# Moving the first factor of a low-rank gate out of a split weight stream

## The chip, the core and the metric

The kernel runs on one core of a Trainium2 chip. The metric is the time of one execution on the device, in microseconds (us). Of the kernel before there are three timed runs, 1939.54, 1939.91 and 1941.91 us, with a median of 1939.91 us, and one profiled execution.

The names used below are those of the profile. PE is TensorE, which multiplies matrices; PEld is its loading of the stationary operand. DVE is VectorE, ACT is ScalarE, POOL is GpSimd and SP is SyncE. SP computes nothing here, but most DMA transfers are issued from its queue, and a smaller part from POOL's. Each engine works through its own instructions in order.

## The reference: what is computed

One step of a decoder layer for 256 prompt rows and 8 sample rows, so 264 columns in all (`NT`), with a model width of 2048. All weights are float32. The input is normalised and modulated by a vector that depends on the conditioning input, giving `h`. One projection `z = h @ w_in` feeds three mixers. The third one, gated linear attention, takes from it queries, keys, values, an output gate and 16 columns `glr`, the first half of a low-rank gate:

```python
h = rmsnorm(x, g_pre_mix) * (1.0 + sc1) + sh1
z = h @ w_in                                   # 2048 x 15376
(z_uv, hq, hf, hi, hg, gq, gk, gv, gr, glr, z_gate) = split(z, offsets)
log_a = log_sigmoid(glr @ gla_w_up + gla_b_up) / GLA_TAU     # 16 -> 512 columns
```

`glr` stands at columns 9216 to 9231 of `w_in`; columns 9232 and on are the merge gates `z_gate`. The mixers' outputs are projected, merged by the gates and projected again, and a squared-ReLU MLP follows (2048 to 8192 and back).

## The kernel before, in words

Activations are kept transposed: 128 model channels on the partitions, the 264 rows as columns. A block is an SBUF buffer of the pool `b` with 28 of them; four channels' tiles of 128 x 264 fill one. `hh` and `hl` hold `h` split in two parts of a reduced float32 form (`fp32r` in the profile), whose sum is `h`; `xT[q]`, q from 0 to 3, holds the unsplit float32 `h` for channel tiles 4q to 4q+3, from which they are made.

**The weight stream.** Nearly all products go through class `Stream` and `granule`. A weight tile of 128 x 4 x 256 or the like is loaded by SP into a `raw` buffer (512 KB), split by ACT into `whi` (L109) and by DVE into `wlo` (L106), and used in three matmuls per 128 x 128 piece: high part by `hh` (L641), high part by `hl` (L642), low part by `hh` (L643), each with 264 columns. 24 of these are a granule. Loads run up to five granules ahead, splits two. `plan()` writes down the order of the weights once, and `zin(c0, width)` is a projection of `width` columns of `w_in` by this path. For `glr` the width is 128: `zin(9216, P)` computes the 16 wanted columns and 112 unwanted ones, in two granules of 24 matmuls.

**The first phase.** Until about 300 us the kernel works in five passes over 2, 2, 4, 4 and 4 of the 16 channel tiles (`CHUNKS`), because each next pass needs its part of the modulation vector first. That is a product of the conditioning rows with `w_ada` (class `First`, L294): plain float32 matmuls, four of them side by side in the array, each with a stationary operand of 32 columns and its own 32 output partitions. Their weights, 256 or 512 KB each, are loaded by SP into blocks. Later modulation vectors are computed likewise, by `rounds` (L362).

**The gate.** `gla_group()` runs after the first phase: two stream projections for queries, two for keys, `zin(9216, P)`, then four for the values, each followed by one plain float32 matmul for 128 columns of the gate (L1030, 16 rows deep: `gla_w_up` by the copied `lr`).

**The background.** The mixers themselves are generators. After each granule `background()` gives two queues of them an allowance (`rate`, set from `RATES` at the start of each stage), so that their small matmuls and their DVE and ACT work lie between the granules; `now` counts granules, and several waits of the sample part of the mixers are counted in it.

**Order.** On PE, SP and POOL the order is as written in the program; on DVE and ACT, in most stages, a scheduler sets it when the program is built, from its own estimates.

Of the kernel before, what the change touches and what calls it, by code (L numbers as in the profile page):

```python
# [15 lines left out]
P = 128  # L16
# [17 lines left out]
SPLIT_BUFS = 6  # L34
NBLK = 28
CHUNKS = (2, 2, 4, 4, 4)
RATES = ((1.8, 0.5), (1.6, 0.5), (1.25, 0.5), (1.0, 0.5))
ST_BUFS = 4
VB_BUFS = 2
N_PRE = 6  # L40
# [17 lines left out]
def hybrid_step_kernel(  # L58
# [27 lines left out]
    def blk(shape=None, dt=F32):  # L86
        shape = shape or [P, 4, NT]
        return blkp.tile(shape, dt, tag="b", name=nm("b"))
# [447 lines left out]
    def blocks(w, k0, nk, c0, width=CW):  # L536
        kc = min(nk, 1024 // width)
        return [(w, k0 + kb, kc, c0, width) for kb in range(0, nk, kc)]

    def plan():  # L540

        out, k0 = [], 0
        for n in CHUNKS:
            for gi in range(0, len(begin), 4 // n):
                out.append((win, k0, n, begin[gi][0], 4 // n * CW))
            k0 += n
        for c0 in (6144, 6400, 6656, 6912):
            out += blocks(win, 0, KT, c0)
        out += blocks(win, 0, KT, 9216, P)
        for s in range(4):  # L550
            out += blocks(win, 0, KT, 7168 + s * CW)
        for n in range(N_BRANCH):
            if n:
                g0 = 5120 if n == 1 else 8192
                for s in range(4):
                    out += blocks(win, 0, KT, g0 + s * CW)
            for m in range(8):
                out += blocks(win, 0, KT, 9232 + n * D + m * CW) + blocks(w_branch[0, n], 0, 8, m * CW)
        for m in range(8):
            out += blocks(w_out[0], 0, KT, m * CW)  # L560
        for f in range(NFB + 1):
            if f < NFB:
                if f == 0:
                    out += blocks(w_mlp_up[0], 0, KT, 0, 2 * CW)
                for m in range(0 if f else 2, FB // CW):
                    out += blocks(w_mlp_up[0], 0, KT, f * FB + m * CW)
            if f:
                for m in range(8):
                    out += blocks(w_mlp_down[0], (f - 1) * (FB // P), FB // P, m * CW)
        return out  # L570
# [217 lines left out]
    order.__exit__(None, None, None)  # L788
    order = tc.manual_schedule(engines=set(every[0:3]))
    order.__enter__()  # L790
    k0 = 0
    for ci, n in enumerate(CHUNKS):
        final = ci == len(CHUNKS) - 1
# [4 lines left out]
        for gi in range(ng):  # L798
# [12 lines left out]
                    S.activation(dst, dst, fn)  # L811
            if ci == 0 and 2 * gi + 8 < KT:
                x_transposed(2 * gi + 8)
            if not final:
                if ci or gi:
                    next(nxt, None)
            else:
                if gi % 4 == 0:
                    rounds.steps()
                    rounds.load()  # L820
                if gi % 3 == 0 and srcs_a:
                    const_a(srcs_a.pop(0))
# [188 lines left out]
    def gla_group():  # L1011
        G = Group()
        G.dv, G.i = 256, 2
        G.q, G.g, G.k, G.v = blk(), blk(), blk(), [blk(), blk()]
        wl = blk([16, 512 + NT])
        wup, lr = wl[:, 0:512], wl[:, 512:512 + NT]
        nc.gpsimd.dma_start(wup, gla_w_up[0])
        for s in range(2):
            z = zin(6144 + s * CW)
            S.copy(pair(G.q, s), z)  # L1020
        for s in range(2):
            z = zin(6656 + s * CW)
            S.activation(pair(G.k, s), z, AF.Copy, scale=GLA_SCALE)
        z = zin(9216, P)
        S.copy(lr, z[0:16, 0, :])
        for s in range(4):
            z = zin(7168 + s * CW)
            S.copy(pair(G.v[s // 2], s % 2), z)
            ps = sm()
            T.matmul(ps[:, 0:NT], wup[:, s * P:(s + 1) * P], lr, start=True, stop=True)  # L1030
            V.tensor_scalar(G.g[:, s, :], ps[:, 0:NT], bupT[:, s:s + 1], None, ALU.add)
        G.s_in = lambda b, h, n: state_gla[0, b, h:h + n].rearrange("h k v -> k h v")
        G.s_out = lambda b, h, n: gla_sample[0, b, h:h + n].rearrange("h k v -> k h v")
# [709 lines left out]
```

## Time and profile before

| quantity | value |
|---|---|
| median of three runs | 1939.91 us |
| the profiled execution's own time | 1938.26 us |
| its span, first to last instruction | 1936.5 us |
| PE busy | 1903.5 us, 98% of the span |
| DVE, ACT, POOL busy | 1186.6, 1002.7, 84.8 us |
| moved by DMA | 442.05 MB, mean 228 GB/s |

An x with a number behind it is a count of instructions. A plain float32 matmul is recorded twice in the trace, so that counts of them are double those of the program. A row of the timeline gives the start, the time from start to end of the whole row, the engine, the line, output and inputs, the shape (partitions by columns of the stationary operand, then the moving operand) and, in brackets, idle time before it and what ended it. Matmuls overlap: each of those of the stream lasts 0.28 us but starts 0.12 us after the one before it, so durations of single matmuls must not be added up; what one costs is seen from the starts.

### The profile page before, as it was taken

The page shows a single profiled execution, that of the slowest core. Times are in us where ns is not written, and L with a number is a line of the kernel's source. Part 1 is how long each engine was busy: PE and PEld are TensorE (multiplying, and loading weights), DVE is VectorE, ACT ScalarE, POOL GpSimd, SP SyncE. Part 2 cuts the span into 40 slices and gives each one's busy share as a digit, 9 for nine tenths or more (in the row PEclk, how much of TensorE's full clock was granted, in tenths as well). Part 3 has the DMA queues.
Part 4 walks back from the last instruction along what each step waited for, and adds up shares of the span by engine and source line. Part 5 has one row for each costly group of instructions (what it writes and reads, how often), then busy time and mean ns, then how long its engine had stood idle before and what let it go on. Part 6 is the DMA issues. An engine that isn't in the chain of part 4 may idle for free.

```text
span 1936.5 us, 42145 instructions
## 1 busy us (share of the span) xinstructions
PE 1903.5 (98%) x17012; PEld 1813.5 (94%) x17012; DVE 1186.6 (61%) x2092; ACT 1002.7 (52%) x1818; POOL 84.8 (4%) x146
## 2 busy tenths in 40 slices
PE   7999999999999999999999999999999999999998
PEld 5889999999999989899999989999999999999997
DVE  4566667686676784555555666545556555555665
ACT  5434454665855755544444555444444545454544
POOL 1000000001101111100000010000000000000000
PEclk9999999999999999999999999999999999999999
DMA  9897786778778778887777846676665656555552
GB/s 334 318 331 252 232 299 205 227 257 263 230 254 253 228 255 262 288 271 250 255 257 230 302 124 214 221 239 185 184 181 179 185 177 184 180 180 182 180 182 100
DMA packets 339395, 442.05 MB, mean 228 GB/s; under 512 B 14946, under 2 KB 281040, under 8 KB 339200
## 3 DMA queue, kind: packets, MB, share of 16 engines
q1 hardware_dynamic: 329136, 409.62, 65.8%
q0 software_dynamic: 8992, 28.48, 4.5%
q8 instruction: 133, 2.18, 0.4%
q10 hardware_dynamic: 1072, 1.25, 0.2%
q14 instruction: 62, 0.51, 0.1%
HBM read 427.60 MB, written 11.70 MB: 227 GB/s over the span
## 4 chain that ended last, share of the span: by engine, by line
PE 95%; DMA 3%; DVE 1%; ACT 1%; issue 0%; SPq 0%; POOL 0%; DVEq 0%; ACTq 0%
PE mm L641 29%; PE mm L642 28%; PE mm L643 28%; PE ada L362 3%; DMA b<-in_w_ada_dram 2%; PE ada L294 1%; DMA vbc<-vs_d 1%; PE sm L833 1%; PE sm L661 1%; PE sm L1190 1%; PE sm L668 1%; DMA b<-in_x_prompt_dram 0%; PE sm L1560 0%; DMA raw<-in_w_in_dram 0%; DVE wlo L106 0%
## 5 line engine op out<-in xcount | busy, mean ns | idle before, releaser
L641 PE MATMUL mm<-b,whi 128*128 128x264 f32 x4624 | 1325.2, 287 | 2.4 <-ACT b L109 1.6
L643 PE MATMUL mm<-b,wlo 128*128 128x264 f32 x4624 | 1311.9, 284 | 4.1 <-DVE wlo L106 2.6
L642 PE MATMUL mm<-b,whi 128*128 128x264 f32 x4624 | 1313.0, 284 | 1.9 <-issue 1.0
L106 DVE TENSOR_TENSOR wlo<-raw,whi 128x512 fp32r<-128x512 f32 x1136 | 776.7, 689 | 561.8 <-ACT whi L109 557.9
L109 ACT CAST whi<-raw 128x512 fp32r<-128x512 f32 x1136 | 696.1, 618 | 741.7 <-PE mm L642 654.8
L641 PEld LDWEIGHTS mm<-b,whi 128*128 128x128 f32 x4624 | 869.8, 188 | 44.7 <-issue 26.7
L643 PEld LDWEIGHTS mm<-b,wlo 128*128 128x128 f32 x4624 | 869.4, 188 | 6.2 <-DVE wlo L106 3.4
L642 PEld LDWEIGHTS mm<-b,whi 128*128 128x128 f32 x4624 | 869.7, 188 | 1.5 <-DVE b L106 1.2
L103 DVE TENSOR_TENSOR b<-b,mm 128x528 f32<-128x528 f32 (+1 forms) x137 | 95.7, 699 | 41.9 <-PE mm L643 41.7
L1087 DVE SCALAR_TENSOR_TENSOR st<-vbc,b,st 128x128 f32<-128x128 f32 (+1 forms) x96 | 34.2, 390 | 59.6 <-DMA vbc<-vs_d 56.2
L1085 ACT ACTIVATE st<-st,fs 128x128 f32<-128x128 f32 (+1 forms) x96 | 37.2, 431 | 53.9 <-DMA st<-in_state_hgrn_dram 27.2
L362 PE MATMUL ada<-araw,cT 128*32 128x512 f32 x296 | 39.8, 601 | 0.0
L294 PE MATMUL ada<-b,cT 128*32 128x256 f32 (+1 forms) x640 | 35.0, 353 | 3.2 <-DMA b<-in_w_ada_dram 3.0
L100 DVE TENSOR_TENSOR b<-b,b 128x512 f32<-128x512 f32 (+1 forms) x47 | 33.8, 740 | 1.3 <-ACT b L1203 1.1
L294 PEld LDWEIGHTS ada<-b,cT 128*32 128x32 f32 x640 | 17.8, 113 | 15.8 <-DMA b<-in_w_ada_dram 7.6
L1088 POOL DMA_DIRECT2D out_dram<-st x32 | 23.5, 735 | 127.7 <-DVE st L1087 122.9
L362 PE MATMUL ada<-b,cT 128*32 128x512 f32 x216 | 26.2, 593 | 0.0
L106 DVE TENSOR_TENSOR b<-gt,b 128x528 fp32r<-128x528 f32 x32 | 22.7, 708 | 3.2
L106 DVE TENSOR_TENSOR b<-b 128x1024 f32<-128x1024 f32 (+1 forms) x24 | 24.3, 1016 | 0.0
L109 ACT CAST whi<-araw 128x512 fp32r<-128x512 f32 x20 | 12.4, 620 | 21.5 <-PE mm L642 17.2
L100 DVE TENSOR_TENSOR gt<-vt 128x528 f32<-128x528 f32 x32 | 22.5, 702 | 0.9 <-ACT vt L1608 0.9
L1614 ACT ACTIVATE b<-vt 128x528 fp32r<-128x528 f32 x32 | 20.7, 648 | 1.0
(345 smaller groups left out, 839.6 us busy)
## 6 DMA issues: line engine op xcount, KB each, us to landing
raw<-in_w_in_dram SPq DMA_DIRECT2D x231, 512.0 KB, 4.7
raw<-in_w_mlp_up_dram SPq DMA_DIRECT2D x128, 512.0 KB, 3.9
raw<-in_w_mlp_down_dram SPq DMA_DIRECT2D x128, 512.0 KB, 3.6
b<-in_w_ada_dram SPq DMA_DIRECT2D x102, 512.0 KB, 6.4
araw<-in_w_ada_dram SPq DMA_DIRECT2D x74, 512.0 KB, 5.7
raw<-in_w_branch_dram SPq DMA_DIRECT2D x48, 512.0 KB, 4.7
raw<-in_w_out_dram SPq DMA_DIRECT2D x32, 512.0 KB, 3.9
b<-in_w_ada_dram SPq DMA_DIRECT2D x32, 256.0 KB, 5.4
```

Of the source, the lines that this page charges most:

```text
L100: V.tensor_tensor(o, a, b, op=ALU.mult)
L103: V.tensor_tensor(o, a, b, op=ALU.add)
L106: V.tensor_tensor(o, a, b, op=ALU.subtract)
L109: S.copy(hi, src)
L294: T.matmul(acc[32 * j:32 * j + 32, 0:n], cT[:, k, :], w[:, n * j:n * j + n], start=k == 0, stop=k == KT - 1)
L362: T.matmul(self.acc[32 * j:32 * j + 32, :], cT[:, k, :], ws[j // 2][:, j % 2 * 512:j % 2 * 512 + 512], start=k == 0, stop=k == KT - 1)
L641: T.matmul(o, a, xh(k + j), start=first and j == 0, stop=False)
L642: T.matmul(o, a, xl(k + j), start=False, stop=False)
L643: T.matmul(o, b, xh(k + j), start=False, stop=last and j == n - 1)
L1085: S.activation(st[:, i, :], st[:, i, :], AF.Copy, scale=fs[:, h0 + i, b:b + 1])
L1087: V.scalar_tensor_tensor(st[:, i, :], v[:, i, :], k[:, h0 + i, NP + b:NP + b + 1], st[:, i, :], ALU.mult, ALU.add)
L1088: nc.gpsimd.dma_start(G.s_out(b, h0, nh), st)
```

## The change

The 16 columns of `glr` leave the stream. In the first pass POOL loads 32 columns of `w_in`, 9216 to 9247, for all 16 channel tiles into a block `low` (128 partitions x 16 x 32). In the fifth step of passes two to five, `low_rank(q)` multiplies four channel tiles of `xT[q]` by their 32 columns each: four plain float32 matmuls with stationary operands of 128 x 32, into four groups of 32 output partitions, so that their sum over the four is left open. DVE adds up the results of the four calls in `lsum` (128 x 264). In `gla_group()` the block `low` is set to zero and `gla_w_up` is loaded four times, at partitions 0, 32, 64 and 96, so that one matmul of 128 rows in place of 16 sums the four groups and multiplies by `gla_w_up`; the 16 unwanted columns of each group meet zeros. `zin(9216, P)` and its copy are gone, and the second entry of `RATES`, the background's allowance during the first two merges of branches, goes from 1.6 to 1.8.

```diff
-RATES = ((1.8, 0.5), (1.6, 0.5), (1.25, 0.5), (1.0, 0.5))
+RATES = ((1.8, 0.5), (1.8, 0.5), (1.25, 0.5), (1.0, 0.5))
...
-        out += blocks(win, 0, KT, 9216, P)
...
+    wl = blk([P, 512 + NT])
+    low, lsum = wl[:, 0:512], wl[:, 512:512 + NT]
+
+    def low_rank(q):
+
+        ps = sm([P, NT])
+        for j in range(4):
+            T.matmul(ps[32 * j:32 * j + 32, :], low[:, 32 * (4 * q + j):32 * (4 * q + j) + 32], xT[q][:, j, :], start=True, stop=True)
+        if q == 0:
+            V.tensor_copy(lsum, ps)
+        else:
+            add(lsum, lsum, ps)
...
+            if ci == 0 and gi == 2:
+                nc.gpsimd.dma_start(low.rearrange("p (k c) -> p k c", c=32), win[:, 9216:9248].rearrange("(k p) c -> p k c", p=P))
+            if ci and gi == 4:
+                low_rank(k0 // 4)
...
-        wl = blk([16, 512 + NT])
-        wup, lr = wl[:, 0:512], wl[:, 512:512 + NT]
-        nc.gpsimd.dma_start(wup, gla_w_up[0])
+
+        nc.gpsimd.memset(low, 0.0)
+        for j in range(4):
+            nc.gpsimd.dma_start(low[32 * j:32 * j + 16, :], gla_w_up[0])
...
-        z = zin(9216, P)
-        S.copy(lr, z[0:16, 0, :])
...
-            T.matmul(ps[:, 0:NT], wup[:, s * P:(s + 1) * P], lr, start=True, stop=True)
+            T.matmul(ps[:, 0:NT], low[:, s * P:(s + 1) * P], lsum, start=True, stop=True)
```

Three places show how instructions move. The first is PE in the second pass, at the first call of `low_rank`, before and after (`mm` is the stream's accumulator, `ada` that of the modulation, `sm` a small PSUM tile; the changed file's lines stand some numbers off).

```order
L641 MATMUL mm_1096<-b_334,whi_975 128x264
L642 MATMUL mm_1096<-b_335,whi_975 128x264
L643 MATMUL mm_1096<-b_334,wlo_976 128x264
L294 MATMUL ada_894<-b_941,cT 32x256 x4
L294 MATMUL ada_894<-b_943,cT 32x256 x4
L294 MATMUL ada_894<-b_983,cT 32x256 x4
```

```order
L642 MATMUL mm_1098<-b_334,wlo_978 128x264
L798 MATMUL sm_1137<-b_273,b_367 32x264 x4
L294 MATMUL ada_896<-b_943,cT 32x256 x4
L294 MATMUL ada_896<-b_945,cT 32x256 x4
L294 MATMUL ada_896<-b_985,cT 32x256 x4
```

The four new matmuls stand directly ahead of a group of modulation matmuls, which have the same kind of shape. The call of the fifth pass stands ahead of such a group too (of L362); those of the third and the fourth pass stand alone between matmuls of the stream, as here in the third:

```order
L641 MATMUL mm_1556<-b_1312,whi_1473 128x264
L642 MATMUL mm_1556<-b_1311,wlo_1474 128x264
L798 MATMUL sm_1594<-b_361,b_367 32x264 x4
L640 MATMUL mm_1604<-b_1311,whi_1505 128x264
L641 MATMUL mm_1604<-b_1312,whi_1505 128x264
```

The second place is POOL's queue, from the last sample rows of the first modulation on, before and after.

```order
L433 CAST b_334<-b_273 128x2x8
L434 TENSOR_TENSOR b_335<-b_273,b_334 128x2x8
L1017 DMA b_3861<-in_gla_w_up_dram 16x512
L927 DMA out_dram<-sqs_4421 64x128
L1116 DMA vs_d<-sqs_4695 32x128
```

```order
L434 TENSOR_TENSOR b_335<-b_273,b_334 128x2x8
L828 DMA b_367<-in_w_in_dram 128x16x32
L1033 MEMSET b_367 128x512
L1035 DMA b_367<-in_gla_w_up_dram 16x512 x4
L944 DMA out_dram<-sqs_4450 64x128
```

The load of the 32 columns follows L434 at once; the zeroing and the four small loads behind it wait for the last `low_rank`, and nothing else of POOL's stands between.

The third place is SP's queue, around the narrow loads for `zin(9216, P)`, before and after.

```order
L325 DMA araw_4349<-in_w_ada_dram 128x1024
L598 DMA raw_4383<-in_w_in_dram 128x8x128
L598 DMA raw_4417<-in_w_in_dram 128x8x128
L598 DMA raw_4471<-in_w_in_dram 128x4x256
L598 DMA raw_4513<-in_w_in_dram 128x4x256
```

```order
L325 DMA araw_4378<-in_w_ada_dram 128x1024
L597 DMA raw_4412<-in_w_in_dram 128x4x256
L597 DMA raw_4446<-in_w_in_dram 128x4x256
L597 DMA raw_4500<-in_w_in_dram 128x4x256
L597 DMA raw_4542<-in_w_in_dram 128x4x256
```

The two narrow loads are gone and the values' weights take their places. Ahead of this point SP's queue has the same transfers in the same order as before.

## The prediction

> **What bounds the kernel now.** I read the page first: shares of the span, and the slices.
>
> ```profile
> span 1936.5 us, 42145 instructions
> PE 1903.5 (98%) x17012; PEld 1813.5 (94%) x17012; DVE 1186.6 (61%) x2092; ACT 1002.7 (52%) x1818; POOL 84.8 (4%) x146
> ...
> DMA  9897786778778778887777846676665656555552
> ```
>
> PE works in all but 33 us of the span; DMA comes near its limit only in the first slices of 48 us. So a change is worth what it does to PE's own work, except where PE idles. That is in the windows (length, PE busy, PEld, DVE, ACT, POOL, granted clock, DMA share, GB/s):
>
> ```profile
> 0.00:100.00 100.00, 84.61 (x876) 71.86 (x876) 50.01 (x114) 51.88 (x91) 6.55 (x19) 0.98 0.93 328
> 300.00:500.00 200.00, 200.00 (x2019) 187.70 (x2019) 145.78 (x303) 118.16 (x234) 18.43 (x28) 1.00 0.74 233
> 500.00:600.00 100.00, 98.46 (x1171) 91.58 (x1170) 73.37 (x134) 70.04 (x138) 13.04 (x20) 1.00 0.79 256
> 600.00:790.00 190.00, 188.82 (x1915) 177.09 (x1914) 126.73 (x235) 115.99 (x240) 28.38 (x43) 1.00 0.79 251
> 790.00:850.00 60.00, 57.41 (x479) 52.74 (x478) 32.98 (x59) 31.33 (x63) 10.69 (x16) 1.00 0.90 300
> ...
> 1400.00:1800.00 400.00, 400.00 (x3295) 400.00 (x3294) 231.56 (x343) 187.86 (x308) 0.00 (x0) 1.00 0.59 181
> ```
>
> The gate's projection lies in the second window, where PE never idles: its matmuls are all on the path. The first 100 us, into which their replacement goes, are another matter, with 15.4 us of idle PE and a DMA share of 0.93. From 500 to 850 us PE idles 1.5 + 1.2 + 2.6 = 5.3 us. The last window is the stream alone: 400 us / 3295 = 0.121 us per matmul.
>
> **Removed.** Two granules of 24 matmuls: 48 x 0.121 = 5.8 us of PE. Their two loads, four splits on ACT and on DVE and a copy go too, but none of that ended a wait of PE in that window, so I count nothing for it.
>
> **Added: sixteen products.** The modulation's products have the same kind of shape, four stationary operands of 128 x 32 side by side. What a stop for them costs is read from the last matmul of the stream before it to the second one after it, less two ordinary steps (0.24 us).
>
> ```profile
> 125.41 0.29 PE L643 MATMUL mm<-b,wlo 128*128 128x264 f32 x1
> 125.63 1.93 PE L294 MATMUL ada<-b,cT 128*32 128x256 f32 x32
> 127.49 0.39 PE L641 MATMUL mm<-b,whi 128*128 128x264 f32 x1
> 127.72 0.28 PE L642 MATMUL mm<-b,whi 128*128 128x264 f32 x1
> ...
> 281.63 0.28 PE L643 MATMUL mm<-b,wlo 128*128 128x264 f32 x1
> 281.84 1.07 PE L362 MATMUL ada<-araw,cT 128*32 128x512 f32 x8
> 282.83 0.39 PE L641 MATMUL mm<-b,whi 128*128 128x264 f32 x1
> 283.06 0.29 PE L642 MATMUL mm<-b,whi 128*128 128x264 f32 x1
> ```
>
> Sixteen matmuls of 256 columns (32 records), four sets of four: 127.72 - 125.41 - 0.24 = 2.07 us. One set of 512 columns: 283.06 - 281.63 - 0.24 = 1.19 us. With a fixed part and one per column, a set of 256 is (2.07 - 1.19) / 2 = 0.44 us and the fixed part 0.31 us. A set of 264 columns is then 0.45 us, and a stop with one alone 0.76 us. By the order, the calls of passes three and four stand alone (1.52 us), those of passes two and five join a group already there (0.45 us each). Together 2.4 us.
>
> That of pass two I take as hidden. It falls into a stretch that transfers pace:
>
> ```profile
> 66.00:103.00 37.00, 35.44 (x346) 29.95 (x345) 22.99 (x39) 12.25 (x21) 0.00 (x0) 1.00 0.98 370
> ...
> 66.19 3.18 SPq L472 DMA_DIRECT2D b<-in_w_ada_dram  x6
> ...
> PE ada L294 <- DMA b<-in_w_ada_dram: 1.3, 1, 1.3
> ```
>
> From 66 us SP issues the weights of the next modulation, the DMA share is 0.98, and PE at last waits 1.3 us for a block of them: longer than the 0.45 us put ahead of it. With that cover gone it would cost 0.45 us. On the path: 1.52 + 0.45 = 2.0 us.
>
> **Changed: four gate matmuls.** They get 128 rows in place of 16 at the same 264 columns. The nearest rows are that matmul now and two full-array float32 products of 128 columns:
>
> ```profile
> 381.46 0.28 PE L643 MATMUL mm<-b,wlo 128*128 128x264 f32 x1
> 381.67 0.71 PE L1030 MATMUL sm<-b 16*128 16x264 f32 x2
> 382.30 0.39 PE L641 MATMUL mm<-b,whi 128*128 128x264 f32 x1
> 382.53 0.29 PE L642 MATMUL mm<-b,whi 128*128 128x264 f32 x1
> ...
> 1060.20 0.28 PE L643 MATMUL mm<-b,wlo 128*128 128x264 f32 x1
> 1060.32 0.60 PE L833 MATMUL sm<-cst,gt 128*128 128x128 f32 x4
> 1060.67 0.37 PE L641 MATMUL mm<-b,whi 128*128 128x264 f32 x1
> 1060.88 0.29 PE L642 MATMUL mm<-b,whi 128*128 128x264 f32 x1
> ```
>
> The former stops the stream for 382.53 - 381.46 - 0.24 = 0.83 us, the latter for 1060.88 - 1060.20 - 0.24 = 0.44 us with 256 columns in all; for 264 that is 0.45 us. So with 128 rows the matmul should cost 0.38 us less. Three of the four stand alone between matmuls of the stream and the fourth in a cluster of other small ones: -1.3 us, with bounds 0 and -1.5 us.
>
> [...]
>
> **Added: the load of 32 columns.** 2048 rows of 128 bytes, 262 KB. No transfer of this trace has such rows throughout. The nearest are POOL's small loads at the start (the first row, of the window 2 to 10 us: packets, MB, share of 16 engines); the second, of 1400 to 1500 us, is 1 KB rows.
>
> ```profile
> q0 software_dynamic: 238, 0.03, 2.7%
> ...
> q1 hardware_dynamic: 18242, 18.11, 59.3%
> ```
>
> The first is 0.027 x 16 x 8 us / 238 = 14.5 ns for packets of 126 bytes in the mean, the second 0.593 x 16 x 100 us / 18242 = 52 ns. With 128 rows for each of 16 engines the load takes 1.9 us of DMA by the first and 6.7 us by the second; I take the first, which is nearest in size.
>
> When it runs matters more. POOL comes free for it at the end of the sample rows, and what is then in the queues ahead of PE is tight:
>
> ```profile
> 27.03 0.38 POOL L434 TENSOR_TENSOR b<-b,b 128x16 fp32r<-128x16 f32 x1
> 28.47 8.49 SPq L598 DMA_DIRECT2D raw<-in_w_in_dram  x5
> q1 hardware_dynamic: 2355, 3.30, 98.7%
> 34.62 3.35 ACT L109 CAST whi<-raw 128x512 fp32r<-128x512 f32 x6
> 37.88 1.09 ACT L807 COPY b<-mm 128x528 f32<-128x528 f32 x2
> PE mm L641 <- ACT b L807: 0.6, 1, 0.6
> ```
>
> The load starts at about 27.5 us. From 28 to 37 us SP's queue alone keeps the DMA engines at 98.7%, among it five weight tiles; ACT splits them as they come, without a gap, and only then copies the accumulator that PE waits for. A load in the same queues makes these tiles later by its own DMA time, ACT with them, and PE by most of it. Nothing gives it back before 66 us, since PE is busy, and the stretch from 66 us starts when PE has come that far. Bounds: 0 (it fits into gaps) and 6.7 us (1 KB price, all exposed). I take 1.3 us, two thirds of 1.9, as tiles have some tenths of slack.
>
> **The rest of the edits** I count at nothing. POOL's zeroing and the four loads of `gla_w_up` run after about 256 us, and the first gate matmul is at 381 us. DVE's four additions are about as long as what goes. `low` keeps one of 28 blocks occupied and `xT` its blocks longer, so that modulation loads wait for a later release; by the order these releases stand one group of matmuls or less behind those of before, and SP reaches them later than that. The faster background moves the same work, 7 granules earlier at the third mixer's end. Without that cover each of these costs as rivals 2 and 3 say.
>
> **Sum**: -5.8 + 2.0 - 1.3 + 1.3 = -3.8 us against the profiled execution's own 1938.26 us (1.8 us around its span): 1934.5 us. The median of the runs shown is 1.65 us above that execution, so 1936.1 us. What this kernel's measurement can tell from no change is about 0.2%, 3.9 us: below 1936.0 counts as faster. The sum lies on that line.
>
> **Rivals.**
>
> 1. *The load is hidden, or the background's waits shrink.* In the window from 790 us PE loses 2.6 us; DVE stands there, in its order, behind values that POOL's transfers bring late:
>
> ```profile
> PE mm L643 <- DVE wlo L106: 2.6, 3, 1.2
> DVE st L1087 <- DMA vbc<-vs_d: 20.0, 6, 9.2
> ```
>
> With the mixer ready earlier these may fall away, and the load may cost nothing. For it: the sample part's end moves ahead of the end of its stage by some granules more. Against it: its waits are for its own transfers, which move along. -5.1 us with a free load and -2.6 more: 1932.2 to 1934.8 us, say 1933.5.
>
> 2. *New waits.* The allowance of 1.8 puts one eighth more background work per granule onto DVE and ACT. For it: DVE was busy 73% from 300 to 500 us. Against it: in that window the allowance was 1.8 already for most of the time, with no idle PE. One or two waits like those 2.6 us: 1938.7 to 1941.3, say 1940 us.
>
> 3. *Slower than before: the small rows are dear.* One mechanism, the load at 28 to 37 us: each row holds an engine for as long as a 1 KB packet, and PE loses all 6.7 us, for -5.1 + 6.7 = +1.6 us: 1941.5 us. The sum turns to slower above 5.1 us of load, 40 ns per row, and by over 0.2% above 9 us, 70 ns. Against it: the 14.5 ns of POOL's own small packets. [...]
>
> 4. *The four products don't run side by side.* Each call would take four times 0.45 us and the sum +1.6 us, 1941.5 us. Against it: L294's rows show the same form.
>
> **Chances.** The sum as worked out, 1934 to 1938.5 us: 0.62, half of it on each side of 1936.0. Rival 1: 0.16. Rival 2: 0.12. Rival 3: 0.08, of which 0.06 by over 0.2%. Rival 4: 0.02. Faster by over 0.2%: 0.31 + 0.16 = 0.47. Slower: 0.06. Within: the other 0.47. The range takes in rival 1 down to 1932.5 and most of rival 2: 1932.5 to 1940.5 us, 0.85 of the cases.
>
> **What the profile after would show.** The products: rows with a 128*32 operand and 264 columns, a stop of about 0.76 us where they stand alone; several microseconds would be rival 4. The gate matmul: a stop near 0.45 us, not 0.83. The load: a queue of POOL's with some 2048 more packets and its share; PE's window 27 to 43 us idle by 1.3 us more than before, and the weights from 66 us issued so much later. The waits of rivals 1 and 2: PE's 5.3 us of idle time from 500 to 850 us. The forecast is wrong if PE's busy time falls by less than 3 or more than 6 us, or if idle time moves by more than 3 us elsewhere.

## The result and the profile after

The changed kernel takes 1950.26 us in the median of four runs (1948.32 to 1951.60), the kernel before beside it 1939.82 us: a ratio of 1.0051, with a 95% interval of 1.0039 to 1.0062. It is slower by 7.6 to 12 us, where 3.8 us less were forecast. The profiled execution of the changed kernel took 1948.32 us, 10.06 us more than that of before. All medians are of executions in the usual state: two far slower ones, of the runs e4 (2308.51 us) and e8 (6247.29 us) below, are left out.

The page of the changed kernel shows first that PE has not become less busy, and that the span has grown by 10.0 us:

```profile
span 1946.5 us, 42119 instructions
PE 1906.0 (98%) x16996; PEld 1815.1 (93%) x16996; DVE 1184.7 (61%) x2093; ACT 999.3 (51%) x1813; POOL 87.8 (5%) x151
```

PE idles 40.5 us, 7.5 more than before, and is busy 2.5 us longer with fewer instructions. Three places in PE's timeline tell where that arises: the first gate matmul (L1046, before L1030), the first product of the next stage (L850, before L833), and the end.

```profile
378.48 0.71 PE L1046 MATMUL sm<-b 128*128 128x264 f32 x2
...
1067.13 0.60 PE L850 MATMUL sm<-cst,gt 128*128 128x128 f32 x4
```

The first gate matmul comes 3.2 us earlier than before (381.67). So in this pair of traces the change has brought what was forecast up to there, and a little more: -5.8 + 2.0 + 1.3 = -2.5 us. (Over all traces it is less, as the part on the load shows.) The next stage starts 6.8 us later than before (1060.32): between these two places 10.0 us were lost, in the second traces of the two kernels 6.9 us. Another 3.2 us went between there and the end (3.0 us in the second traces). The windows show both losses (columns as in the prediction):

```profile
740.00:755.00 15.00, 11.57 (x67) 10.64 (x66) 6.84 (x12) 7.81 (x19) 2.14 (x3) 0.89 0.60 203
755.00:790.00 35.00, 32.81 (x240) 28.48 (x240) 15.81 (x35) 20.33 (x48) 3.95 (x6) 0.95 0.67 211
...
400.00:850.00 450.00, 437.05 (x4681) 406.55 (x4680) 296.06 (x574) 271.83 (x564) 65.67 (x99) 0.99 0.78 252
1400.00:1800.00 400.00, 400.00 (x3282) 400.00 (x3281) 230.44 (x341) 186.52 (x307) 0.00 (x0) 1.00 0.61 180
```

From 400 to 850 us PE idles 450 - 437.05 = 13.0 us, against 5.3 before: 7.7 us more. Here the granted clock is below one as well, 0.89 and 0.95 in the two windows quoted; in windows of 5 us it is 0.73 and 0.93 from 745 to 755 us and 0.66 from 780 to 785 us, and one in all others of the stage. Summed as 5 us x (1 - clock), that is 3.4 us of lost clock. Before, no window of this stage was below one. In the last stage PE is busy throughout, and yet 400 us hold 3282 matmuls in place of 3295: 0.1219 us each against 0.1214.

What PE waited for, by the two longest new rows of the table of waits:

```profile
PE sm L1247 <- ACT b L1250: 3.4, 1, 3.4
PE sm L1292 <- ACT b L1283: 2.2, 2, 1.8
```

The longest of them, in the timelines of PE and ACT:

```profile
742.01 0.59 PE L1246 MATMUL sm<-b,b 128*128 128x256 f32 x2
746.04 0.70 PE L1247 MATMUL sm<-b,b 128*128 128x256 f32 x2 [3.43 <-ACT b L1250]
...
743.32 0.91 ACT L1101 ACTIVATE st<-st,fs 128x256 f32<-128x256 f32 x2 [2.60 <-DMA st<-in_state_gla_dram]
744.13 1.12 ACT L109 CAST whi<-raw 128x512 fp32r<-128x512 f32 x2
745.16 0.82 ACT L1250 ACTIVATE b<-sm,ft 128x256 f32<-128x256 f32 x2
```

PE has two steps of the third mixer to do, one behind the other with no matmuls of the stream between them. The second needs an accumulator that ACT has to copy out (L1250). ACT stands at another instruction, the scaling of a sample's recurrent state (L1101), whose transfer lands only at 743.3 us; two splits follow, and the copy comes at 745.2. So PE doesn't wait for its own producer's work, but for a transfer that stands ahead of it in ACT's queue.

### The profile page after: what moved, and what is told of

It reads as the page before. It is cut to its first block, busy times and chain, and to the rows that moved or that the text cites. A ratio compares the mean times of both kernels' runs of the same rounds, so it can differ in the third digit from the quotient of the medians.

```text
span 1946.5 us, 42119 instructions
## 1 busy us (share of the span) xinstructions
PE 1906.0 (98%) x16996; PEld 1815.1 (93%) x16996; DVE 1184.7 (61%) x2093; ACT 999.3 (51%) x1813; POOL 87.8 (5%) x151
## 4 chain that ended last, share of the span: by engine, by line
PE 90%; DMA 4%; issue 1%; DVE 1%; ACT 1%; POOL 1%; SPq 0%; ACTq 0%; DVEq 0%; POOLq 0%
PE mm L640 28%; PE mm L641 27%; PE mm L642 27%; PE ada L362 3%; PE ada L294 1%; DMA b<-in_w_ada_dram 1%; DMA st<-in_state_gla_dram 1%; PE sm L850 1%; DMA vbc<-vs_d 1%; ACT whi L109 1%; DMA st<-in_state_hgrn_dram 1%; DVE wlo L106 1%; PE sm L660 0%; PE sm L1206 0%; PE sm L667 0%
## 5 line engine op out<-in xcount | busy, mean ns | idle before, releaser
L1101 ACT ACTIVATE st<-st,fs 128x128 f32<-128x128 f32 (+1 forms) x96 | 36.9, 429 | 64.2 <-DMA st<-in_state_hgrn_dram 31.0
L1103 DVE SCALAR_TENSOR_TENSOR st<-vbc,b,st 128x128 f32<-128x128 f32 (+1 forms) x96 | 34.0, 390 | 58.8 <-DMA vbc<-vs_d 50.6
L362 PE MATMUL ada<-araw,cT 128*32 128x512 f32 x296 | 40.1, 611 | 0.0
L100 DVE TENSOR_TENSOR b<-b,b 128x512 f32<-128x512 f32 (+1 forms) x47 | 33.7, 741 | 0.1
L294 PEld LDWEIGHTS ada<-b,cT 128*32 128x32 f32 x640 | 19.3, 119 | 13.9 <-DMA b<-in_w_ada_dram 5.1
L1104 POOL DMA_DIRECT2D out_dram<-st x32 | 23.5, 735 | 118.5 <-DVE st L1103 116.2
L362 PE MATMUL ada<-b,cT 128*32 128x512 f32 x216 | 26.2, 593 | 0.0
L109 ACT CAST whi<-araw 128x512 fp32r<-128x512 f32 x20 | 12.4, 619 | 22.3 <-PE mm L641 20.5
L100 DVE TENSOR_TENSOR gt<-vt 128x528 f32<-128x528 f32 x32 | 22.4, 702 | 0.9 <-ACT vt L1624 0.9
L362 PEld LDWEIGHTS ada<-b,cT 128*32 128x32 f32 x216 | 6.8, 111 | 15.5 <-issue 14.8
```

Source lines behind the costliest of these rows:

```text
L100: V.tensor_tensor(o, a, b, op=ALU.mult)
L109: S.copy(hi, src)
L294: T.matmul(acc[32 * j:32 * j + 32, 0:n], cT[:, k, :], w[:, n * j:n * j + n], start=k == 0, stop=k == KT - 1)
L362: T.matmul(self.acc[32 * j:32 * j + 32, :], cT[:, k, :], ws[j // 2][:, j % 2 * 512:j % 2 * 512 + 512], start=k == 0, stop=k == KT - 1)
L1101: S.activation(st[:, i, :], st[:, i, :], AF.Copy, scale=fs[:, h0 + i, b:b + 1])
L1103: V.scalar_tensor_tensor(st[:, i, :], v[:, i, :], k[:, h0 + i, NP + b:NP + b + 1], st[:, i, :], ALU.mult, ALU.add)
```

## The experiments

Idle time is that of PE from 400 to 850 us, clock loss the sum of 5 us x (1 - granted clock) from 380 to 870 us, and the last column the count of matmul records from 1400 to 1800 us. These three are from one profiled execution each, which can lie several us from the median beside it (e16's took 1951.94 us); two traces of one kernel differ by up to 2.0 us in the first and by 1.7 us in the second. The ratio is to runs of the kernel before on the same chip, in the same job; jobs are compared by ratio, since the kernel before itself went from 1939.8 to 1941.3 us.

| kernel | time us | ratio, 95% interval | idle us | clock loss us | matmuls |
|---|---|---|---|---|---|
| before, first trace | 1938.26 | | 5.3 | 0 | 3295 |
| before, again (c0) | 1941.25 | | 7.3 | 0 | 3294 |
| changed | 1950.26 | 1.0051, 1.0039 to 1.0062 | 13.0 | 3.4 | 3282 |
| changed, again | 1951.73 | | 12.4 | 1.7 | 3282 |
| e1: changed, allowance 1.6 | 1942.84 | 1.0012, 1.0003 to 1.0021 | 10.0 | 3.4 | 3295 |
| e2: before, allowance 1.8 | 1958.52 | 1.0097, 1.0081 to 1.0112 | 16.4 | 10.2 | 3290 |
| e3: before, no projection | 1940.42 | 1.0002, 0.9991 to 1.0013 | 10.2 | 5.1 | 3292 |
| e4: changed, states not waited for | 1934.33 | 0.9970, 0.9959 to 0.9982 | 3.3 | 0 | 3291 |
| e5: before, states not waited for | 1936.82 | 0.9981, 0.9972 to 0.9990 | 2.6 | 0 | 3291 |
| e7: e1, four granules | 1945.53 | 1.0036, 1.0023 to 1.0048 | 9.7 | 3.4 | 3294 |
| e8: before, four granules | 1941.39 | 1.0007, 0.9997 to 1.0016 | 6.8 | 0 | 3296 |
| e9: changed, states on GpSimd | 1952.12 | 1.0060, 1.0047 to 1.0073 | 13.3 | 3.4 | 3283 |
| e10: e1, states on GpSimd | 1946.67 | 1.0027, 1.0016 to 1.0038 | 10.1 | 1.7 | 3292 |
| e11: before, states on GpSimd | 1945.99 | 1.0032, 1.0022 to 1.0043 | 8.8 | 0 | 3298 |
| e12: changed, stores late | 1975.74 | 1.0186, 1.0171 to 1.0201 | 23.4 | 11.9 | 3283 |
| e13: e1, stores late | 1952.54 | 1.0066, 1.0052 to 1.0080 | 10.6 | 3.5 | 3292 |
| e14: before, stores late | 1949.41 | 1.0049, 1.0037 to 1.0061 | 11.1 | 6.8 | 3298 |
| e15: changed, blocks moved | 1950.11 | 1.0045, 1.0030 to 1.0060 | 15.8 | 5.1 | 3288 |
| e16: changed, allowance 1.5 | 1946.27 | 1.0028, 1.0018 to 1.0039 | 11.6 | 6.8 | 3295 |
| e17: changed, allowance 1.7 | 1945.62 | 1.0026, 1.0016 to 1.0037 | 9.6 | 5.1 | 3292 |

### The parts of the change apart (c0, e1, e2, e3)

The change has two parts that reach the stage where the time was lost: the projection that leaves the stream, and the background's allowance of 1.8 steps per granule.

```diff
 e1, on the changed kernel        e2, on the kernel before
-RATES = ((1.8, 0.5), (1.8, 0.5)  -RATES = ((1.8, 0.5), (1.6, 0.5)
+RATES = ((1.8, 0.5), (1.6, 0.5)  +RATES = ((1.8, 0.5), (1.8, 0.5)
 e3, on the kernel before
-        out += blocks(win, 0, KT, 9216, P)
...
-        z = zin(9216, P)
```

c0, the kernel before once more:

> The kernel before once more, for a second trace beside the others. In its last stage (1400 to 1800 us) the first trace counts 3295 matmuls, the changed kernel's 3288 less 0.5%: 0.1214 against 0.1220 us each. If the pace belongs to the layout of the buffers, this trace has 0.1214 again; if it varies from run to run, another value, up to 0.1220. Time 1939 to 1942 us either way.

e1:

> The changed kernel with the second stage's allowance back at 1.6. Theory A, the allowance: two steps of the mixer in one granule, with no stream between, made the 7.7 us of new PE idle time and the dips of the clock from 400 to 850 us; they go, and the time is 1936 to 1940 us. Rival B, the alignment: the mixer, some 20 us earlier, meets the sample part's transfers at another place whatever the allowance: the idle time stays at 10 us or more and the time at 1946 to 1951 us.

e2:

> The kernel before with the second stage's allowance at 1.8 and nothing else changed. Theory A: it takes the new idle time with it, 1945 to 1950 us. Rival B: 1938 to 1942 us, idle time from 400 to 850 us near the 5.3 us of before.

e3:

> The kernel before without the projection of columns 9216 to 9343 and its two loads (the low-rank factor is then taken from the projection of k, so the gate's values are others); allowance 1.6. The price of the removed work by itself: 5.8 us by the count of matmuls, 1934 us, if nothing else moves (theory A). Rival B: the third mixer meets the transfers of the sample states at other places, PE idles from 400 to 850 us by several us more than 5.3, and the time is 1937 us or above.

Measured: the allowance of 1.8 by itself makes the kernel before 18.8 us slower by the ratio (17.3 us between the medians), more than the whole change does, with 16.4 us of idle time and 10.2 us of clock loss. Theory A had expected the sign and a quarter to half of the size. Taken back in the changed kernel it returns 7.4 us, not the 10 to 14 that theory A expected: 10.0 us of idle time stay. And e3 shows that rival B holds as well. With only the projection left out, 48 matmuls less, the kernel is no faster at all: the 5.8 us come back as 10.2 us of idle time and 5.1 us of clock loss. So each of the two parts, made alone, makes PE wait in this stage. Not everything that moves the background does: e8, below, changes when states are used and costs nothing. The windows of e2 and e3 for the stage:

```profile
400.00:850.00 450.00, 433.62 (x4601) 401.16 (x4600) 291.75 (x558) 267.82 (x552) 65.86 (x99) 0.98 0.77 250
```

```profile
400.00:850.00 450.00, 439.79 (x4687) 409.82 (x4686) 295.51 (x553) 273.33 (x562) 63.88 (x96) 0.99 0.77 250
```

A wait of e1 at 540 us shows the same thing as that of 742 us in the changed kernel, this time with the stream itself behind it. DVE's rows are left out; PE's wait is for the split that follows ACT's row at 540.91:

```profile
534.91 0.69 ACT L1101 ACTIVATE st<-st,fs 128x128 f32<-128x128 f32 x2
540.60 0.40 ACT L1101 ACTIVATE st<-st,fs 128x128 f32<-128x128 f32 x1 [5.01 <-DMA st<-in_state_hgrn_dram]
540.91 0.60 ACT L109 CAST whi<-raw 128x512 fp32r<-128x512 f32 x1
...
542.47 0.39 PE L642 MATMUL mm<-b,wlo 128*128 128x264 f32 x1 [2.35 <-DVE wlo L106]
```

In the second trace of the kernel before (c0), ACT waits for the same state at the same time, longer, and PE does not idle:

```profile
534.59 0.98 ACT L1085 ACTIVATE st<-st,fs 128x128 f32<-128x128 f32 x3
541.18 0.40 ACT L1085 ACTIVATE st<-st,fs 128x128 f32<-128x128 f32 x1 [5.60 <-DMA st<-in_state_hgrn_dram]
541.49 0.60 ACT L109 CAST whi<-raw 128x512 fp32r<-128x512 f32 x1
...
538.29 0.60 PE L305 MATMUL sm<-cst,gt 128*128 128x128 f32 x4
538.82 1.07 PE L362 MATMUL ada<-araw,cT 128*32 128x512 f32 x8
```

PE has a group of the modulation's products there, 1.5 us that need no split, and it has it just then. So the kernel before has the same waits on ACT, and happens to have other work for PE at most of them. That is also how the totals over the whole kernel read, first of before, then of the changed kernel:

```profile
ACT st L1085 <- DMA st<-in_state_hgrn_dram: 27.2, 9, 8.4
ACT st L1085 <- DMA st<-in_state_gla_dram: 26.6, 11, 6.4
DVE st L1087 <- DMA vbc<-vs_d: 56.2, 20, 9.2
```

```profile
ACT st L1101 <- DMA st<-in_state_hgrn_dram: 31.0, 8, 6.5
ACT st L1101 <- DMA st<-in_state_gla_dram: 27.1, 10, 5.1
DVE st L1103 <- DMA vbc<-vs_d: 50.6, 17, 7.6
```

Before 27.2 + 26.6 + 56.2 = 110 us, after 31.0 + 27.1 + 50.6 = 109 us; the same lines' waits for something else, or for nothing that the profile names, add 3 and 14 us. In e1 the three are 104 us, in e2 106, with 10.0 and 16.4 us of idle PE. So the time that these engines wait for transfers doesn't tell the kernels apart; where they wait does.

### Taking the waits away (e4, e5)

From this came theory C: it is the transfers of the sample states, at the head of ACT's and DVE's queues, that make PE wait. The rival D: the mixer's steps, packed closer, by themselves. The edit takes away what is waited for, in both kernels; the loads of the states are left out, so that the outputs of the samples are others, and 8 MB less are moved.

```diff
-            nc.gpsimd.dma_start(st, G.s_in(b, h, nh))
...
-    S.activation(st[:, i, :], st[:, i, :], AF.Copy, scale=fs[...])
+    S.activation(st[:, i, :], k[:, h0 + i, 0:dv], AF.Copy, scale=fs[...])
...
-    V.scalar_tensor_tensor(st[:, i, :], v[:, i, :], k[...], st[:, i, :], ALU.mult, ALU.add)
+    V.scalar_tensor_tensor(st[:, i, :], k[:, h0 + i, 0:dv], k[...], st[:, i, :], ALU.mult, ALU.add)
```

> The changed kernel (allowance 1.8) without waits for the sample states: their loads are left out, ScalarE scales k in their place and VectorE adds k in place of the loaded values, so the sample outputs are others; all other instructions keep their order. Theory C: ScalarE and VectorE stand in order behind a state's transfer, and the splits and copies behind them make PE wait; the idle time of PE from 400 to 850 us falls from 13.0 to 4 us or less, no granted clock below 0.9 stays there, and the time is 1933 to 1938 us. What may stay are waits between two steps of the mixer in one granule, 1 to 2 us each. Rival D: the steps of the mixer alone, packed closer, make the idle time: 9 us or more stay, and 1943 us or above.

> The kernel before with the same edit. Theory C: idle time from 400 to 850 us falls from 5.3 to 3 us or less, 1935 to 1939 us. The difference to the changed kernel with this edit is then the change's work on PE alone: 3.8 us less by the prediction's sum, so by theory C the changed kernel is 2 to 6 us the faster of the two; by rival D it stays 5 us or more the slower.

Measured: 1934.33 us for the changed kernel, 1936.82 us for the one before. Theory C holds here, rival D falls: with the waits gone and the allowance still at 1.8, idle time drops from 13.0 to 3.3 us, no window of the stage is below full clock, and 16 of the 1950 us go. The edit also takes 8 MB off the DMA queues, so that weights could come sooner too; but in the changed kernel ACT's splits wait for weights only 5.4 us in this stage, and for states ACT waits 58 us. The stage's windows, first of e4, then of e5:

```profile
400.00:850.00 450.00, 446.68 (x4800) 418.48 (x4799) 310.13 (x589) 286.68 (x581) 45.24 (x70) 1.00 0.74 242
```

```profile
400.00:850.00 450.00, 447.45 (x4799) 418.59 (x4798) 307.83 (x580) 283.37 (x568) 45.33 (x70) 1.00 0.75 244
```

The changed kernel is now the faster one, by 2.5 us in the medians, within the 2 to 6 us that were expected. The two intervals overlap (0.9959 to 0.9982 and 0.9972 to 0.9990), but of the 60 pairs of an execution of each, it is the faster in 53. The traces say more. In e5 the last group of the modulation ahead of the gate, and the first gate matmul:

```profile
376.77 1.06 PE L362 MATMUL ada<-araw,cT 128*32 128x512 f32 x8
383.80 0.71 PE L1030 MATMUL sm<-b 16*128 16x264 f32 x2
...
1070.72 0.49 PE L833 MATMUL sm<-cst,gt 128*128 128x128 f32 x3
```

And in e4:

```profile
381.51 1.06 PE L362 MATMUL ada<-araw,cT 128*32 128x512 f32 x8
382.50 0.71 PE L1046 MATMUL sm<-b 128*128 128x264 f32 x2
...
1068.65 0.60 PE L850 MATMUL sm<-cst,gt 128*128 128x128 f32 x4
```

Ahead of the gate e4 is 4.7 us behind, at the gate 1.3 us ahead, and at the next stage 2.1 us ahead. The part from 377 to 1070 us is worth 4.7 + 2.1 = 6.8 us (the first of e5's last rows lacks a record, which is 0.1 us of that), where the prediction had 5.8 + 1.3 = 7.1 us. The 4.7 us ahead of it are what the load and the sixteen products cost in this pair, where the prediction had 2.0 + 1.3 = 3.3 us.

### Three attempts to keep the gain (e7 to e14)

If late states cost the time, states used later, or fetched earlier, should bring it back, with the whole computation. First, a state is used at the earliest four granules after its fetch, in place of three (`FETCHED`): e7 on the changed kernel with 1.6, e8 on the one before.

> The changed kernel with the allowance at 1.6 and the sample states used four granules after their fetch at the earliest, in place of three; the computation is the reference's. Theory C: each state is used later behind its fetch, ScalarE waits less for it; idle time from 400 to 850 us falls to 5 us or less and the time to 1933 to 1937 us, faster than before by 0.2% or more. Rival D: no change against the kernel with 1.6 alone, 1942 to 1944 us.

> The kernel before with the same four granules and nothing else. Theory C: idle time from 400 to 850 us 3 us or less, 1936 to 1940 us; the changed kernel with 1.6 and four granules is then 3 to 5 us the faster of the two. Rival D: as before, 1940 to 1942 us.

Both are misses: no gain, and e7 2.4 thousandths slower than e1. The granules of that rule are counted in the written order of the program, while the fetch starts when GpSimd's queue reaches it; ACT's waits for states grew, from 57 us in e1 to 71 us.

Second, the three operations on a state go to GpSimd, so that neither ACT nor DVE stands behind a state's transfer:

```diff
-    S.activation(st[:, i, :], st[:, i, :], AF.Copy, scale=fs[...])
-    V.scalar_tensor_tensor(st[:, i, :], v[:, i, :], k[...], st[:, i, :], ALU.mult, ALU.add)
+    nc.gpsimd.tensor_tensor(v, v, kb, ALU.mult)
+    nc.gpsimd.tensor_tensor(st, st, fs[...].to_broadcast(shape), ALU.mult)
+    nc.gpsimd.tensor_tensor(st, st, v, ALU.add)
```

> The changed kernel (allowance 1.8) with the three operations on each sample state on GpSimd in place of ScalarE and VectorE: the same results, but now only GpSimd's queue stands behind the transfer of a state. Theory C: idle time of PE from 400 to 850 us 5 us or less, no dip of the clock there, 1933 to 1937 us: what the kernel without waits showed (1935.4 us), with the whole computation. [...]

> The same edit on the changed kernel with the allowance at 1.6. Theory C: 1933 to 1937 us as well; with the waits for the states gone the allowance hardly matters, and the two lie within 2 us of each other. Rival: the closer packing at 1.8 costs by itself, and this one is 3 us or more the faster.

> The same edit on the kernel before. Theory C: 1936 to 1939 us (1936.8 us without the waits), 2 to 4 us above the changed kernel with the edit, which is then what the change's own work on PE is worth. Rival: 1940 us or above, no faster than before.

All three miss theory C. The waits for states on ACT and DVE are gone, and the lost time is not. PE's waits for DVE's split from 400 to 850 us add up to 7.1 us in e9, for 2.1 in the changed kernel. DVE's split of the stream takes longer on the average, and some of its operations very much longer, as e9 shows (the group of the split, 689 ns before, and one operation of the same shape and kind):

```profile
L106 DVE TENSOR_TENSOR wlo<-raw,whi 128x512 fp32r<-128x512 f32 x1132 | 827.2, 738 | 582.3 <-ACT whi L109 577.2 <-PE sm L667 1.3 <-PE mm L641 1.1
...
709.89 3.28 DVE L100 TENSOR_TENSOR b<-b,b 128x512 f32<-128x512 f32 x1
```

The split takes 738 ns in e9 and 735 ns in e11, where GpSimd has the operations on the states (in e9 128.1 us of them, L1102 to L1104), and 689 ns each in the changed kernel and in the one before, where it has none. In e9 the operations of the second row's group (L100, of two blocks) take 1037 ns on the average, in the changed kernel 741 ns. By what these operations of DVE are lengthened is not shown.

e10 is 5.4 us faster than e9, as its rival had it. So the allowance of 1.8 costs something even where no state is waited for on ACT or DVE; whether by closer packing or by these longer operations of DVE is not shown.

Third, in GpSimd's queue each state's store is put one step later, behind the next fetch:

```diff
+            if out:
+                nc.gpsimd.dma_start(*out.pop())
...
-            nc.gpsimd.dma_start(G.s_out(b, h0, nh), st)
+            out.append((G.s_out(b, h0, nh), st))
```

> The changed kernel (allowance 1.8); in GpSimd's queue the store of a sample state stands one step later, behind the next state's fetch. The fetch then doesn't wait any more for VectorE to finish the state before, and lands some 6 us sooner against its use; the results are the same. Theory C: ScalarE's waits for states of 3 to 8 us shrink below 3 us, PE's idle time from 400 to 850 us falls to 8 us or less, and the time to 1940 to 1945 us (the last stage's pace of 0.1220 stays). Rival: VectorE's waits for the values, which stay where they are, decide: idle time 11 us or more, 1947 us or above.

> The same edit on the changed kernel with the allowance at 1.6 (1942.8 us with 10.0 us of idle time). Theory C: idle time 5 us or less, 1934 to 1938 us, faster than before. Rival: 1941 us or above.

> The same edit on the kernel before. Theory C: idle time 3 to 5 us, 1937 to 1940 us; little is to be had, since its waits of ScalarE mostly lie where PE has splits in hand. Rival: 1941 us or above.

This is the largest miss: all three are slower, e12 by 25 us against the changed kernel. Putting the stores later did not bring the states earlier. There are four buffers for states, a fetch has to wait for one that PE's products have read and the store has left, and a store that is issued later frees it later. In e12 GpSimd's fetches wait for products and, which the changed kernel's table does not have, for the stores themselves; DVE's wait for the values goes from 50.6 to 78.7 us:

```profile
POOL st L1075 <- PE sm L667: 186.6, 11, 27.6
POOL st L1075 <- DMA out_dram<-st: 39.6, 6, 8.7
...
DVE st L1105 <- DMA vbc<-vs_d: 78.7, 21, 7.0
```

The wait that the edit was to remove, of the stores for DVE in GpSimd's queue, does shrink, from 117 to 19 us; the fetches' waits grow from 180 to 244 us. So the part of theory C that e4 showed stands, PE's time is lost behind transfers on ACT and DVE. What makes these transfers late is not shown: e12 exchanged one wait in GpSimd's queue for another, and no run had more buffers.

### Trend or scatter (e16, e17), and the last stage (changed again, e15)

> The changed kernel with the second stage's allowance at 1.5. ScalarE and VectorE wait for the sample transfers about as long in all kernels so far (100 to 115 us together), before as after; what differs is where. Theory E, the meeting places: the time depends on the allowance without a trend, and lies anywhere from 1935 to 1947 us. Theory F, the packing: less of the mixer per granule leaves more stream between its steps, and the time falls further from 1950 us (1.8) over 1943 us (1.6) to 1937 to 1941 us.

> The changed kernel with the allowance at 1.7. Theory F: between the times of 1.6 and 1.8, 1944 to 1949 us, with the wait of the mixer's state products (3.4 us at 1.8) about half as long. Theory E: outside of that, below 1943 or above 1950 us, or at one end.

Over allowances of 1.5, 1.6, 1.7 and 1.8 the ratios to before are 1.0028, 1.0012, 1.0026 and 1.0051. There is no falling trend below 1.6: theory F is out at its lower end. From 1.6 to 1.8 the times rise in order, as theory F has it, and e17 is within its range; but the wait of 3.4 us that was to be halved is gone there. The places of the waits differ each time: e17's longest is 4.1 us at 802.6 us, at an instruction (L1292) where the changed kernel has none over 1.8. So neither theory is shown. None of the four is faster than before.

> The changed kernel once more, for a second trace. Its last stage ran at 0.1220 us per matmul in the first trace, all other kernels so far at 0.1214 to 0.1216. If that belongs to where its buffers lie, 0.1220 again; if to that execution, 0.1215. The idle time of PE from 400 to 850 us should be 12 to 14 us again, with the clock below 0.8 behind the longest waits.

> The changed kernel with one block of the pool taken for an instant (GpSimd zeroes one column) ahead of the last stages: every instruction stays in its order, and from there on the blocks lie at other addresses. If the layout sets the last stage's pace, it leaves 0.1220 us per matmul for some other value, 0.1214 to 0.1218, and the time falls by up to 3 us, to 1947 to 1950 us. If the pace comes from elsewhere, 0.1220 and 1950 us.

The second trace of the changed kernel has 3282 matmuls again (the 3288 in c0's expectation is a wrong count), and that of the kernel before 3294 for 3295, so the slow last stage belongs to the changed kernel. Its idle time is 12.4 us, within what was expected. The edit of e15 is one line that takes a block for an instant:

```diff
+    nc.gpsimd.memset(blk()[:, 0, 0:1], 0.0)
     x1 = [[blk([P, 1024]) for _ in range(2)] for _ in range(2)]
```

No instruction changes its place, but the blocks lie elsewhere from there on, and the count rises to 3288, half of the way. In e9 and e12, 3283. So by this one trace the placing of the buffers moves the pace; by what mechanism is open. The time of e15 did not fall (1950.11 us, and its stage from 400 to 850 us, where nothing differs, idled 15.8 us in its trace), so these 1 to 2 us are seen in the count alone.

## Why the prediction was wrong

The forecast was the sum of what the change adds to and takes from PE's own work, and its terms came out nearly as worked out, but for the load and pass two's call. What failed is the sentence under "the rest of the edits", that the faster background moves the same work and costs nothing, and with it rival 2, which priced new waits at one or two of 2.6 us. Twice, at the load and in the stage of the gate, the prediction priced a wait of PE at its length, and had no term for the clock behind it.

**What bounds the kernel.** That PE bounds it is right. That the stage of the gate has no idle PE, and so any matmul removed there is time gained, was right for the windows quoted, up to 500 us, and was taken too far: the stage runs on to 850 us, with 110 us of waits on ACT and DVE for the sample part. They are in the table of waits of before (20.0 us of them were quoted); I read them as harmless because PE did not idle.

**Removed, 5.8 us.** Right: between the last modulation group and the first gate matmul e4 gains 4.7 + 1.3 = 6.0 us on e5. As time of the whole kernel it was wrong: e3, which does only this, gains nothing.

**The products, 2.0 us.** Right, but for 0.4 us in this pair of traces. In the changed kernel the calls of passes three and four stop the stream alone, here the second of them:

```profile
122.95 0.29 PE L642 MATMUL mm<-b,wlo 128*128 128x264 f32 x1
123.16 0.66 PE L798 MATMUL sm<-b,b 128*32 128x264 f32 x8
123.75 0.39 PE L640 MATMUL mm<-b,whi 128*128 128x264 f32 x1
123.97 0.28 PE L641 MATMUL mm<-b,whi 128*128 128x264 f32 x1
```

123.97 - 122.95 - 0.24 = 0.78 us (0.76 forecast). The four sit side by side: rival 4 is out. Pass two's call is hidden in this pair, though not in the median of all traces (below), and the whole of passes three to five, from 100 to 375 us, costs 2.4 us, by the starts of the same instructions in both traces.

**The gate matmul, -1.3 us.** Right:

```profile
390.56 0.29 PE L642 MATMUL mm<-b,wlo 128*128 128x264 f32 x1
390.68 0.61 PE L1046 MATMUL sm<-b 128*128 128x264 f32 x2
390.93 0.48 PE L640 MATMUL mm<-b,whi 128*128 128x264 f32 x1
391.25 0.28 PE L641 MATMUL mm<-b,whi 128*128 128x264 f32 x1
```

391.25 - 390.56 - 0.24 = 0.45 us, as forecast, for 0.83 before. The two others that stand alone stop the stream for 0.45 us as well, and the fourth, next to a modulation group, 0.96 us for 1.15: together -1.4 us.

**The load, +1.3 us.** Right in place and in the length of the wait; what that wait does to the clock was left out. It takes less of DMA than forecast, 5.5% of 16 us, 0.9 us for 1.9, in the window from 24 to 40 us:

```profile
q1 hardware_dynamic: 3589, 5.22, 93.4%
q0 software_dynamic: 80, 0.26, 5.5%
...
PE mm L640 <- ACT b L820: 1.4, 1, 1.4
```

PE waits 1.4 us at the copy where it waited 0.6, and up to 47 us loses 0.6 us. In the second trace of the changed kernel the wait is 1.9 us and the clock is at 0.66 from 40 to 45 us, another 1.7 us; the loss up to there is 3.9 us against c0:

```profile
40.00:45.00 5.00, 4.34 (x23) 4.34 (x24) 0.94 (x3) 2.27 (x6) 0.00 (x0) 0.66 1.03 355
```

The edits of all other runs lie behind the first phase, so that eight traces have the first phase of the kernel before and twelve that of the changed one. The wait at the copy is 0.6 or 0.7 us in the eight and 1.0 to 3.1 us in the twelve, with a median of 1.9: 1.3 us more, as forecast. But half clock follows it in six of the twelve and in none of the eight, at 1.7 us each. In the medians the stretch with the load, from 24 to 55 us of before, is 2.0 us longer in the twelve, that with pass two's call, from 55 to 98 us, 0.6 us, and that with the other calls, from 98 to 282 us, 2.4 us. So load and products cost 5.0 us, where 3.3 were forecast. The first pair showed 2.8 by luck: at the modulation group that the prediction shows at 281.84 us, the changed kernel's first trace (284.6) is the earliest of the twelve (up to 289.3).

Rival 3 is out: the load takes 7 ns a row. It is not recorded as the 2048 small packets, though, on which the forecast and rival 3 were worked out: the trace has 64 packets of 4096 bytes and 16 of 4 bytes. That 1.9 us was of the right order is luck.

**The background, counted at nothing.** This is the step that failed. The prediction said of rival 2 that the allowance had been 1.8 already from 300 to 500 us with no idle PE. It had, but the sample states are transferred mostly after 500 us, so that stretch could tell nothing of what two steps per granule meet there. The change's own work on PE is worth about -2 us (-6.0 for the projection, 5.0 for load and products, -1.4 for the gate matmuls; e4 against e5: -2.5). In the first pair of traces the stage gave 10 us back, 7.7 of idle time and 3.4 of clock, less what the gate matmuls gain there. The runs apart show where this comes from: the allowance alone costs 17 to 19 us (e2), and the projection's 5.8 us come back as waits and clock with the allowance as it was (e3). Rival 2 had the right kind and a quarter to half of the size, since it counted two waits of the size that the trace of before showed, and knew no price for the clock that falls behind a wait. The last 3.2 us, most of them the pace of the last stage, belong to no step of the prediction; a row to forecast them from was not there.

Of what the prediction named as showing it wrong, the first came: PE's busy time was to fall by 3 to 6 us, and rose by 2.5. In it are the lower clock and the slower last stage, which the page counts as busy.

## What to carry to other kernels

An engine that waits long without stopping the bottleneck engine is not idle at no price: it is slack that the present order happens to cover. Before a change that moves work against such waits (here 110 us of them on the two engines that feed PE), list them, and look for what PE has in hand at each; a change that is worth 2 us on PE must not shift them. And where a change comes with a tuned constant, run the constant alone on the old kernel: here it cost 18.8 us by itself. And a stretch that several runs share should be compared over all their traces: here one pair showed 2.8 us and the medians of twenty traces 5.0.

## What the runs showed of the hardware

**The clock fell behind short gaps.** In the twenty traces PE has 82 gaps of 1 us or more between 380 and 880 us. Within 3.5 us behind their end the granted clock falls to 0.50 after none of the 35 below 1.5 us, after 18 of the 31 from 1.5 to 2.5 us and after 15 of the 16 longer ones (where two gaps stand ahead of one fall, both are counted). What one costs, summed over windows of 1 us as 1 - clock, is 1.7 or 3.4 us in most of them. The longest of the changed kernel's first trace, at 742.6 us, and its windows:

```profile
740.00:745.00 5.00, 2.61 (x14) 2.00 (x12) 3.04 (x7) 2.40 (x6) 0.00 (x0) 1.00 0.69 247
745.00:750.00 5.00, 3.96 (x18) 3.75 (x19) 2.41 (x4) 1.82 (x5) 1.66 (x3) 0.73 0.70 233
```

So a gap of 3.4 us cost 5.1: the clock is at 0.50 from 747.32 to 750.74 us, which is the other 1.7 us.

**The length of a gap alone did not decide it.** In each trace with several stretches of half clock, these start on one grid with a step of 3.413 us: those of the changed kernel's first trace, at 747.32 and 781.46 us, are ten steps apart, three of e2's, at 609.32, 786.82 and 841.42 us, 52 and 16, and the first and last of the first trace of before, at 23.86 and 1935.32 us, 560. Laid on that grid from 380 to 880 us, all 27 windows at full clock in which PE was busy for less than 45% by the profile are followed by half clock, 3 of the 13 from 45 to 60%, and none of the 2845 others. So a gap of 1.78 us ahead of the same instruction (L1292) cost 1.7 us of clock in the changed kernel's first trace, where it left 36% to its window, and nothing in the second, where it fell across two windows of 69 and 72%.

**The small rows of this load were cheap.** 2048 rows of 128 bytes took 0.9 us of 16 DMA engines, 7 ns a row, by the share above; put on its 64 packets of 4096 bytes, 32 rows each, that is 220 ns apiece.

**The same matmuls run at 0.1214 or 0.1219 us** in the two kernels, with PE busy throughout; with other block addresses one trace of the changed kernel (e15) had 0.1217. The mechanism is open.
